# A gate/up stage that starts its first two products over four blocks instead of three, with their copies in one large tile

## The chip, the cores and the metric

The kernel runs on one core of one Trainium2 chip. The metric is the time of one execution on the device, in microseconds (us). The core has TensorE (matmuls into eight PSUM banks), VectorE, ScalarE, GpSimd and SyncE (SP), each with its own queue of instructions. DMA engines move data between HBM and SBUF.

## What is computed

One layer of a streaming encoder over 1024 tokens of width 1024: a SwiGLU feed-forward, a mixer of two head groups, a second feed-forward, and a final RMSNorm. The change touches the two feed-forwards alone, whose inner width is 2816:

```python
def _swiglu(x, w_gate, w_up, w_down):
    return (jax.nn.silu(x @ w_gate) * (x @ w_up)) @ w_down

h = _rmsnorm(x, ffn1_norm[l])
x = x + 0.5 * _swiglu(h, ffn1_w_gate[l], ffn1_w_up[l], ffn1_w_down[l])
# ... mixer ...
h = _rmsnorm(x, ffn2_norm[l])
x = x + 0.5 * _swiglu(h, ffn2_w_gate[l], ffn2_w_up[l], ffn2_w_down[l])
```

All is float32. A product of two float32 matrices is made of three matmuls, high by high, high by low and low by high, from operands that are split into a high half (a cast on ScalarE) and a low half (a subtraction on VectorE).

## The kernel before, in words

**Seven products.** The tokens are cut into two halves of 512 and the width into two halves of 512, so the normed input is four quarters A11, A12, A21, A22. Each pair of column blocks of a weight matrix is multiplied with it in seven products instead of eight (Strassen's scheme in Winograd's form). The inputs are A11, A12, A22 and the sums S1 = A21 + A22, S2 = S1 - A11, S3 = A22 - A21 (made as A22 - S2 after S2's update in place), S4 = A12 - S2. The products are numbered 1 to 7; the table at line 47 tells which input each takes: 1 A11, 2 A12, 3 S4, 4 A22, 5 S1, 6 S2, 7 S3.

**Blocks.** `gate_up` (L276) goes over 22 blocks: 11 pairs of columns, each first for the gate ("g"), then for up ("u"). A block has two weight rows of 0.5 MB (`row`, L287). `weight` (L299) makes the weights of one product from them: for products 1, 2 and 3 a split alone, for 5, 6, 7 and 4 a subtraction in place and then a split. `product` (L328) is 12 matmuls: four quarters of the inner width, three matmuls each. The blocks use PSUM banks by product: X for 1, 6, 7 and 4, which add up in one bank and are read after each; Z for 5 and 3; W for 2.

**Draining.** `evac` (L342) reads a bank after a product. After 1, 5 and 6 it copies it with ScalarE to an SBUF tile (L348). After 2, 3 and 7 VectorE adds bank and copy, in place in the copy (L362); a gate block's sum then goes through Silu, an up block's is multiplied with it (L368) and stored in HBM. After 4, `finish` (L375) makes the sums that the next stage reads.

**Order.** The list `steps` (L388) begins with product 1 of blocks 0 to 2, then product 2 of them, then 5, 6, 3, 7, 4 of them block by block; `early` is 3. From block 3 on, a block's seven products follow each other, with product 4 of the block before behind product 1. `run` (L395) goes through this list: it makes weights six steps ahead, issues the product, and drains it. With `hold=6` the first six products are not drained until the seventh step. The functions `s1`, `s2`, `s4`, `s3`, `a22` of `h_units` (L224) make the five late inputs; the list `STAGES` (L50) says at which steps they are issued. This order is the program's; the framework then places each engine's instructions by priority (the program's order) and by when it expects them to be ready, so that the order in a queue is fixed before the run but is not the text's.

**Buffers.** There are 14 large tiles ("big", four times 128x512), 17 tiles of 128x528 ("xt"), 5 weight rows ("raw"), 8 tiles of split weights ("unit") and 8 PSUM banks. The seven inputs take 14 large tiles when all are there, a high and a low one each. The two rows of block 2 lie in a large tile too (`extra`, L292), until its last weights have been made. The input x lies in 16 of the 17 xt tiles; x[0][0..3] come free after S2's subtractions (L257), x[0][4..7] after S4.

**After the gate/up stage** the down stage (`down`, L425) does the same with activations as inputs; it is not changed. Its loads are ordered behind the last product 1 of the gate/up stage.

Of the kernel before, what the change touches and what calls it, by code (L numbers as in the profile page):

```python
# [10 lines left out]
F32 = mybir.dt.float32  # L11
# [6 lines left out]
P = 128  # L18
D = 1024
S = 1024  # L20
T = 512
# [25 lines left out]
A_OF = {1: "A11", 2: "A12", 3: "S4", 4: "A22", 5: "S1", 6: "S2", 7: "S3"}  # L47
UNITS = ("A11", "A12", "A22", "S1", "S2", "S3", "S4")
GROUPS = ((0, 4), (4, 8), (8, 11))
STAGES = (5, 5, 7, 10, 12)  # L50


class Net:
# [222 lines left out]
    def gate_up(self, n):  # L276
        nc, d = self.nc, self.d
        self.actd = {
            (u, g): self.dp.tile([q1 - q0, P, T], F32, name=f"act{n}{u}{g}")
            for u in UNITS  # L280
            for g, (q0, q1) in enumerate(GROUPS)
        }
        blocks = [(p, m) for p in range(NP) for m in ("g", "u")]
        rows, sil, fence, extra = {}, {}, {}, []
        early = 3

        def row(b, i):  # L287
            p, m = blocks[b]
            if (b, i) not in rows:
                if b == early - 1:  # L290
                    if not extra:
                        extra.append(self.big.tile([P, 4, T], F32, tag="b", name=f"r{m}"))  # L292
                    rows[b, i] = extra[0][:, 2 * i : 2 * i + 2]
                else:
                    rows[b, i] = self.rp.tile([P, 2, T], F32, tag="r", name=f"r{m}{i}")
                nc.sync.dma_start(rows[b, i].rearrange("p a t -> p (a t)"), d[f"{m}{n}"][2 * p + i])
            return rows[b, i]

        def weight(b, M):  # L299
            r0 = row(b, 0)  # L300
            if M in (1, 2):
                src = r0[:, M - 1]
            else:
                r1 = row(b, 1)
                if M == 5:
                    src = r1[:, 0]
                    nc.vector.tensor_sub(src, r1[:, 0], r0[:, 0])
                elif M == 6:
                    src = r1[:, 0]
                    nc.vector.tensor_sub(src, r1[:, 1], r1[:, 0])  # L310
                elif M == 7:
                    src = r0[:, 0]
                    nc.vector.tensor_sub(src, r1[:, 0], r0[:, 0])
                elif M == 4:
                    src = r0[:, 1]
                    nc.vector.tensor_sub(src, r0[:, 1], r1[:, 0])
                else:
                    src = r1[:, 1]
            w = self.unit("wu")
            name = self.split(w[:, 0], w[:, 1], src, after=fence.get("early"))  # L320
            if (b, M) == (early - 1, 2):
                fence["early"] = name
            return w

        bank, part = {}, {}
        place = {1: "X", 6: "X", 7: "X", 4: "X", 5: "Z", 3: "Z", 2: "W"}

        def product(b, M, w):  # L328
            ch = place[M]
            new = M in (1, 2, 5)  # L330
            if new:
                bank[b, ch] = self.fpsum("p" + ch)
            ps = bank[b, ch]
            hh, hl = self.h[A_OF[M]]
            ins = self.mm3(
                ps, [(w[:, 0, k * P : k * P + P], w[:, 1, k * P : k * P + P], hh[:, k], hl[:, k]) for k in range(4)], start=new
            )
            self.last_mm = ins.ins.name
            if (b, M) == (len(blocks) - 1, 1):
                self.gate = self.last_mm  # L340

        def evac(b, M):  # L342
            p, m = blocks[b]
            ps = bank[b, place[M]]
            key = {1: "m1", 5: "m5", 6: "u2"}.get(M)
            if key:
                part[b, key] = self.tmp(key)
                nc.scalar.copy(part[b, key], ps)  # L348
                return
            if M == 4:  # L350
                if m == "g":
                    s = self.tmp("s21")
                    self.table(s, ps, AF.Silu)
                    sil[p, "A21"] = s
                else:
                    s = sil[p, "A21"]
                    nc.vector.tensor_mul(s, ps, s)
                    finish(p)
                return
            key, name = {2: ("m1", "A11"), 3: ("u2", "A12"), 7: ("m5", "A22")}[M]  # L360
            t = part.pop((b, key))
            nc.vector.tensor_add(t, ps, t)  # L362
            if m == "g":
                self.table(t, t, AF.Silu)
                sil[p, name] = t
            else:
                s = sil[p, name]
                nc.vector.tensor_mul(s, t, s)  # L368
                store(p, name, s)

        def store(p, u, t):
            g = next(i for i, (q0, q1) in enumerate(GROUPS) if q0 <= p < q1)
            nc.sync.dma_start(self.actd[u, g][p - GROUPS[g][0]], t)

        def finish(p):  # L375
            a11, a12, a21, a22 = (sil.pop((p, q)) for q in ("A11", "A12", "A21", "A22"))
            s1 = a21
            nc.vector.tensor_add(s1, a21, a22)
            store(p, "S1", s1)
            s2, s3, s4 = (self.tmp(q) for q in ("S2", "S3", "S4"))  # L380
            nc.vector.tensor_sub(s2, s1, a11)
            store(p, "S2", s2)
            nc.vector.tensor_sub(s3, a22, s2)
            store(p, "S3", s3)
            nc.vector.tensor_sub(s4, a12, s2)
            store(p, "S4", s4)

        steps = [(b, M) for M in (1, 2) for b in range(early)]  # L388
        steps += [(b, M) for M in (5, 6, 3, 7, 4) for b in range(early)][:-1]
        for b in range(early, len(blocks)):  # L390
            steps += [(b, 1), (b - 1, 4)] + [(b, M) for M in (2, 5, 6, 3, 7)]
        steps.append((len(blocks) - 1, 4))
        return steps, weight, product, evac

    def run(self, steps, weight, product, evac, ahead, hold=0, stages=(), at=(), early=()):  # L395
# [525 lines left out]
def layer(ctx, tc, d):  # L921
    net = Net(ctx, tc, d)
    nc = tc.nc
# [15 lines left out]
    with ExitStack() as f1:  # L939
        net.ffn_pools(f1)  # L940
        net.load_x(d["x"])
        r[0] = net.rsqrt(net.squares(0))
        ps = net.squares(1)
        first, kinds = net.h_units(0, r)
        first()
        r[1] = net.rsqrt(ps)
        net.run(*net.gate_up(1), ahead=6, hold=6, stages=list(zip(STAGES, kinds)))

        accs = [None, None]
        count = [0, 0]  # L950
        h = [None, None]

        pending = []

        def tail(c, k):
            if c and k < 4:
                pending.append(k)
                return
            finish(c, k)

        def finish(c, k):
            ins = nc.scalar.dma_start(x1[c, :, k], net.x[c][k])
            after = net.wcast["qk0"] if c and k < 4 else None
            if after:
                net.after(ins, after)
            accs[c] = net.square(net.x[c][k], accs[c], net.tmp, after)
            count[c] += 1
            if c == 0 and count[c] == KT:
                r[0] = net.rstd(accs[0], net.unit("sp"), net.fpsum)

        def early():
            h[0] = net.norm(0, 8, r[0], net.last_mm)

        net.down(1, d["x"], tail, order, ((4, 5), early))
# [34 lines left out]
    with ExitStack() as f2:  # L1009
# [5 lines left out]
            r2[1] = net.rsqrt(net.total(sums, net.fpsum, False))  # L1015

        stages = [(1, stats2)] + list(zip(STAGES, h2[1]))
        net.run(*net.gate_up(2), ahead=6, hold=6, stages=stages)

        accs3 = [None, None]  # L1020
        count3 = [0, 0]
# [82 lines left out]
```

## Time and profile before

| what | value |
|---|---|
| median of 3 runs | 1691.99 us (1691.86 to 1694.9) |
| the profiled execution | 1692.0 us, of which its span is 1690.2 us |
| mean granted clock of TensorE | 0.994 |
| TensorE matmuls busy | 1647.9 us, 97% |
| VectorE busy | 1110.1 us, 66% |
| ScalarE busy | 679.2 us, 40% |
| mean HBM traffic | 118 GB/s |

The profile is one execution. Times in a timeline are microseconds from the start of the span. PE is TensorE, DVE VectorE, ACT ScalarE, SP SyncE. A matmul's row is longer than the distance to the next one, since matmuls overlap in the pipeline and their ends are modelled: what a matmul costs is read from the distance between starts. A bracket behind a row tells how long the engine was idle before it and what it then waited for. Names in a row are the program's tiles: "pX<-A11h,wu" is a matmul into an X bank from the high half of A11 and a weight tile, "L212 ... wu<-rg,wu" the low half of a split.

### The profile page before, as it was taken

To read this page: it belongs to the slowest core of one execution; us is meant where nothing else is said; L and a number is where in the kernel's file an instruction comes from. 1 tells how busy PE (TensorE), PEld (TensorE's weight loads), DVE (VectorE), ACT (ScalarE), POOL (GpSimd) and SP (SyncE) were. 2 spreads that over 40 slices of the span, in tenths; PEclk is the share of its full clock that TensorE was granted. 3 is DMA by queue.
4 is the path that set the end of the run, shared out by engine and by line. 5 is a ranking of instruction groups with operands and counts; after the bars stand their busy time and mean duration, and the time that the engine had idled before them with its cause. 6 is when DMAs were issued, how large, how long until landed. Compare 5 with 4: busy or idle time off the path is not lost.

```text
span 1690.2 us, 19875 instructions
## 1 busy us (share of the span) xinstructions
PE 1647.9 (97%) x7314; PEld 1342.9 (79%) x7314; DVE 1110.1 (66%) x1771; ACT 679.2 (40%) x1155; POOL 60.5 (4%) x79
## 2 busy tenths in 40 slices
PE   6999999999999999999999999999999999999997
PEld 3688888888888877888877887788888888888875
DVE  7976565666569668942636539966666665579584
ACT  5643333333444445521423314633333333444452
POOL 0000000000000000100305200000000000000000
PEclk9999999999999999999999999999999999999998
DMA  5142322332795332230310342143233331893331
GB/s 187 61 139 94 106 100 94 112 101 81 246 329 187 110 113 89 61 95 13 106 38 13 121 166 75 69 132 105 100 105 102 111 119 57 279 326 111 112 119 50
DMA packets 95697, 200.07 MB, mean 118 GB/s; under 512 B 10472, under 2 KB 14568, under 8 KB 95600
## 3 DMA queue, kind: packets, MB, share of 16 engines
q1 hardware_dynamic: 89104, 187.21, 33.1%
q10 hardware_dynamic: 6496, 11.60, 1.8%
q8 instruction: 57, 0.93, 0.2%
q14 instruction: 40, 0.33, 0.1%
HBM read 145.78 MB, written 52.99 MB: 118 GB/s over the span
## 4 chain that ended last, share of the span: by engine, by line
PE 92%; DVE 5%; ACT 1%; DMA 1%; issue 1%; SPq 0%; DVEq 0%; ACTq 0%
PE pX L138 14%; PE pX L140 14%; PE pX L139 14%; PE pZ L139 7%; PE pZ L140 7%; PE pZ L138 7%; PE pW L138 3%; PE pW L139 3%; PE pW L140 3%; PE pg L140 3%; PE pg L138 3%; PE pg L139 3%; PE pt L593 2%; PE pt L594 2%; PE pt L592 2%; DVE x L236 1%
## 5 line engine op out<-in xcount | busy, mean ns | idle before, releaser
L209 ACT CAST au<-as 128x512 fp32r<-128x512 f32 x154 | 95.9, 623 | 208.1 <-PE pX L140 104.6
L212 DVE TENSOR_TENSOR au<-as,au 128x512 fp32r<-128x512 f32 x154 | 106.0, 688 | 108.5 <-ACT au L209 108.2
L212 DVE TENSOR_TENSOR wu<-rg,wu 128x512 fp32r<-128x512 f32 x154 | 106.0, 689 | 95.3 <-ACT wu L209 95.0
L209 ACT CAST wu<-ru 128x512 fp32r<-128x512 f32 x154 | 95.4, 622 | 154.9 <-PE pX L140 65.0
L212 DVE TENSOR_TENSOR wu<-ru,wu 128x512 fp32r<-128x512 f32 x154 | 105.6, 687 | 56.5 <-ACT wu L209 56.0
L138 PE MATMUL pX<-au,wu 128*128 128x512 f32 x352 | 137.2, 390 | 0.0
L209 ACT CAST wu<-rg 128x512 fp32r<-128x512 f32 x154 | 95.5, 621 | 103.3 <-issue 53.1
L139 PE MATMUL pX<-au,wu 128*128 128x512 f32 x352 | 137.0, 389 | 0.0
L140 PE MATMUL pX<-au,wu 128*128 128x512 f32 x352 | 137.0, 389 | 0.0
L212 DVE TENSOR_TENSOR wu<-wq,wu 128x512 fp32r<-128x512 f32 x154 | 105.0, 684 | 4.2 <-ACT wu L209 4.1
L209 ACT CAST wu<-wq 128x512 fp32r<-128x512 f32 x154 | 94.4, 615 | 7.6 <-DMA wq<-d 4.9
L138 PE MATMUL pX<-A11h,wu 128*128 128x512 f32 x176 | 70.1, 399 | 7.8 <-ACT wu L209 6.3
L138 PEld LDWEIGHTS pX<-au,wu 128*128 128x128 f32 x352 | 66.1, 188 | 14.3 <-ACT wu L209 0.7
L140 PEld LDWEIGHTS pX<-au,wu 128*128 128x128 f32 x352 | 66.1, 188 | 13.7
L139 PEld LDWEIGHTS pX<-au,wu 128*128 128x128 f32 x352 | 66.1, 188 | 13.7
L139 PE MATMUL pZ<-S1l,wu 128*128 128x512 f32 x176 | 69.4, 394 | 2.9 <-DVE S1l L212 2.9
L139 PE MATMUL pX<-A11l,wu 128*128 128x512 f32 x176 | 70.2, 399 | 0.9 <-DVE A11l L212 0.9
L138 PE MATMUL pX<-S2h,wu 128*128 128x512 f32 x176 | 68.7, 390 | 2.4 <-ACT m L348 2.4
L138 PE MATMUL pZ<-S1h,wu 128*128 128x512 f32 x176 | 68.0, 394 | 1.6 <-ACT S1h L209 1.3
L140 PE MATMUL pX<-A11h,wu 128*128 128x512 f32 x176 | 69.5, 396 | 0.0
L138 PE MATMUL pW<-A12h,wu 128*128 128x512 f32 x176 | 69.2, 393 | 0.0
L139 PE MATMUL pW<-A12l,wu 128*128 128x512 f32 x176 | 69.2, 393 | 0.0
(258 smaller groups left out, 4117.5 us busy)
## 6 DMA issues: line engine op xcount, KB each, us to landing
rg<-g SPq DMA_DIRECT2D x44, 512.0 KB, 3.6
ru<-u SPq DMA_DIRECT2D x44, 512.0 KB, 3.6
wq<-d SPq DMA_DIRECT2D x88, 256.0 KB, 5.2
x<-x SPq DMA_DIRECT2D x64, 256.0 KB, 5.3
as<-act1S SPq DMA_DIRECT2D x44, 256.0 KB, 3.4
as<-act2S SPq DMA_DIRECT2D x44, 256.0 KB, 3.3
act1S<-S SPq DMA_DIRECT2D x33, 256.0 KB, 2.1
as<-act1A SPq DMA_DIRECT2D x33, 256.0 KB, 4.5
```

The source lines that it names most:

```text
L138: nc.tensor.matmul(out, wh, hh, start=start and i == 0, stop=False, skip_group_check=True)
L139: nc.tensor.matmul(out, wh, hl, start=False, stop=False, skip_group_check=True)
L140: ins = nc.tensor.matmul(out, wl, hh, start=False, stop=stop and i == n - 1, skip_group_check=True)
L209: cast = nc.scalar.copy(hi, src)
L212: (eng or nc.vector).tensor_sub(lo, src, hi.bitcast(F32))
L236: nc.vector.scalar_tensor_tensor(x, x, g, r[c], op0=ALU.mult, op1=ALU.mult)
L592: nc.tensor.matmul(ps, hh, wh, start=k == 0, stop=False)
L593: nc.tensor.matmul(ps, hh, wl, start=False, stop=False)
L594: nc.tensor.matmul(ps, hl, wh, start=False, stop=k == KT - 1)
```

## The change

The early part grows by two products: products 1 and 2 of block 3 come behind those of blocks 0 to 2 and ahead of product 5 of block 0. From the later part they are taken out, so block 3 goes on with product 4 of block 2 and its own 5, 6, 3, 7. The order of later blocks stays.

Nothing is held back: `hold` is 0, and each product is drained when it is done. The copies of product 1 of blocks 0 to 3 go into four quarters of one large tile (`first`) and not into xt tiles. The adds of product 2 of these blocks read this copy and write a new xt tile.

The steps at which S2, S4, S3 and A22 are issued are moved by one or two (`STAGES`), and the mark that keeps later weights behind the early ones (`fence`) moves to product 2 of block 3.

```diff
-STAGES = (5, 5, 7, 10, 12)
+STAGES = (5, 6, 9, 12, 14)
...
-        rows, sil, fence, extra = {}, {}, {}, []
+        rows, sil, fence, extra, first = {}, {}, {}, [], []
         early = 3
...
-            if (b, M) == (early - 1, 2):
+            if (b, M) == (early, 2):
                 fence["early"] = name
...
             if key:
-                part[b, key] = self.tmp(key)
+                if M == 1 and b <= early:
+                    if not first:
+                        first.append(self.big.tile([P, 4, T], F32, tag="b", name="m"))
+                    part[b, key] = first[0][:, b]
+                else:
+                    part[b, key] = self.tmp(key)
                 nc.scalar.copy(part[b, key], ps)
                 return
...
-            t = part.pop((b, key))
-            nc.vector.tensor_add(t, ps, t)
+            t = src = part.pop((b, key))
+            if M == 2 and b <= early:
+                t = self.tmp("m1")
+            nc.vector.tensor_add(t, ps, src)
...
-        steps = [(b, M) for M in (1, 2) for b in range(early)]
+        steps = [(b, M) for M in (1, 2) for b in range(early)] + [(early, 1), (early, 2)]
         steps += [(b, M) for M in (5, 6, 3, 7, 4) for b in range(early)][:-1]
         for b in range(early, len(blocks)):
-            steps += [(b, 1), (b - 1, 4)] + [(b, M) for M in (2, 5, 6, 3, 7)]
+            steps += ([] if b == early else [(b, 1)]) + [(b - 1, 4)]
+            steps += [(b, M) for M in ((5, 6, 3, 7) if b == early else (2, 5, 6, 3, 7))]
...
-        net.run(*net.gate_up(1), ahead=6, hold=6, stages=list(zip(STAGES, kinds)))
+        net.run(*net.gate_up(1), ahead=6, hold=0, stages=list(zip(STAGES, kinds)))
...
-        net.run(*net.gate_up(2), ahead=6, hold=6, stages=stages)
+        net.run(*net.gate_up(2), ahead=6, hold=0, stages=stages)
```

## Rows read from the trace of the kernel before

**Rows 1.** The page, busy time: engine, us, share of the span, instructions.
```profile
PE 1647.9 (97%) x7314; PEld 1342.9 (79%) x7314; DVE 1110.1 (66%) x1771; ACT 679.2 (40%) x1155; POOL 60.5 (4%) x79
```

**Rows 2.** Busy time by stage: stretch, its length, engines, granted clock, DMA share, GB/s.
```profile
44.17:67.16 22.99, 18.86 (x73) 13.00 (x73) 22.77 (x38) 14.98 (x26) 0.00 (x0) 1.00 0.03 12
...
1053.58:1075.09 21.51, 18.64 (x74) 12.89 (x72) 21.31 (x36) 15.34 (x27) 0.00 (x0) 1.00 0.04 13
...
100.00:400.00 300.00, 300.00 (x1325) 248.47 (x1324) 185.62 (x285) 111.96 (x191) 0.00 (x0) 1.00 0.32 105
```

**Rows 3.** Timeline of TensorE, first feed-forward: start, length, instruction, count, idle before.
```profile
43.94 0.39 PE L140 MATMUL pW<-A12h,wu 128*128 128x512 f32 x1
45.61 0.73 PE L138 MATMUL pZ<-S1h,wu 128*128 128x512 f32 x2 [1.28 <-ACT S1h L209]
...
48.87 0.50 PE L139 MATMUL pZ<-S1l,wu 128*128 128x512 f32 x1 [0.54 <-DVE S1l L212]
...
56.15 0.50 PE L138 MATMUL pX<-S2h,wu 128*128 128x512 f32 x1 [1.22 <-ACT m L348]
...
67.16 0.39 PE L138 MATMUL pZ<-S4h,wu 128*128 128x512 f32 x1
...
75.32 0.39 PE L138 MATMUL pX<-S3h,wu 128*128 128x512 f32 x1
...
83.48 0.61 PE L138 MATMUL pX<-A22h,wu 128*128 128x512 f32 x2
83.94 0.39 PE L138 MATMUL pX<-A11h,wu 128*128 128x512 f32 x1
...
97.08 0.39 PE L138 MATMUL pZ<-S1h,wu 128*128 128x512 f32 x1
```

**Rows 4.** Timeline of TensorE, second feed-forward.
```profile
1033.73 0.80 PE L138 MATMUL pX<-A11h,wu 128*128 128x512 f32 x1 [3.35 <-ACT wu L209]
...
1040.15 0.39 PE L138 MATMUL pX<-A11h,wu 128*128 128x512 f32 x1
...
1053.58 0.61 PE L138 MATMUL pZ<-S1h,wu 128*128 128x512 f32 x2
...
1075.09 0.39 PE L138 MATMUL pZ<-S4h,wu 128*128 128x512 f32 x1
...
1105.01 0.39 PE L138 MATMUL pZ<-S1h,wu 128*128 128x512 f32 x1
```

**Rows 5.** Timeline of VectorE, first feed-forward.
```profile
41.57 2.07 DVE L236 SCALAR_TENSOR_TENSOR x<-x,cols,rstd 128x512 f32<-128x512 f32 x3
...
50.00 0.68 DVE L257 TENSOR_TENSOR x<-x,x 128x512 f32<-128x512 f32 x1
...
57.46 1.88 DVE L362 TENSOR_TENSOR m<-pW,m 128x512 f32<-128x512 f32 x3
...
83.60 2.49 DVE L212 TENSOR_TENSOR A22l<-x,A22h 128x512 fp32r<-128x512 f32 x4
86.00 0.68 DVE L362 TENSOR_TENSOR m<-pX,m 128x512 f32<-128x512 f32 x1
...
97.35 0.69 DVE L362 TENSOR_TENSOR m<-pW,m 128x512 f32<-128x512 f32 x1 [0.33 <-PE pW L140]
```

**Rows 6.** Timeline of ScalarE, first feed-forward.
```profile
42.16 0.62 ACT L209 CAST wu<-rg 128x512 fp32r<-128x512 f32 x1 [1.60 <-PE pW L140]
...
55.51 0.59 ACT L348 COPY m<-pX 128x512 f32<-128x512 f32 x1
```

**Rows 7.** Timeline of VectorE, second feed-forward.
```profile
1089.78 2.49 DVE L212 TENSOR_TENSOR A22l<-x,A22h 128x512 fp32r<-128x512 f32 x4
```

**Rows 8.** Busy time of a stretch, columns as in rows 2.
```profile
1034.00:1039.00 5.00, 5.00 (x12) 3.70 (x13) 5.00 (x9) 3.02 (x7) 0.00 (x0) 0.50 0.70 277
```

## The prediction

> **What bounds the kernel now.** I read the page first. TensorE is busy for 97% of the span and VectorE for 66% [rows 1], so the time can only fall where TensorE waits. The table by stage says where that is: in a steady stretch of the first gate/up, TensorE is busy for 300.00 of 300.00 us, but at the start of each gate/up it has real holes, and there VectorE is busy for all but 0.22 us of the stretch [rows 2]. Time gained there is gained at the end, for no hole follows until the stage is over.
>
> The size of the holes comes from the timeline of TensorE. With no hole, 36 matmuls (the three S4 products) take 75.32 - 67.16 = 8.16 us, that is 0.2267 us each and 2.72 us for a product of 12. In the first feed-forward the last early product starts its last matmul at 43.94, so TensorE is free at 44.17. The six products on S1 and S2 should take 16.32 us, but the first S4 matmul starts at 67.16: 22.99 us, so 6.67 us are lost [rows 3]. In the second feed-forward the same six run from 1053.58 to 1075.09, 21.51 us, so 5.19 us are lost [rows 4]. Together 11.86 us: more than this the change can't bring here.
>
> The timelines of VectorE and ScalarE tell why. VectorE begins the S1 chain (norm, add, split, for four quarters) only at 41.57 and works without a pause; S1's last quarter and S2 keep TensorE waiting in small steps [rows 3, 5]. Then (0,6) waits 1.22 us for a copy of the first product, made at 55.51 because the copies were held back and need a slot of the 17 [rows 3, 6].
>
> **The change part by part.** Write (b,M) for product M of block b.
>
> *Two products move forward.* (3,1) and (3,2) now run before S1 is needed. That is 24 matmuls, 5.44 us, in each feed-forward, put into holes of 6.67 and 5.19 us. Their weights cost VectorE one split each. The other two-step weights (difference and split) of (1,6) and (2,6) fall behind the S1 chain, so before S1 VectorE has 16 operations and not 18. Their weight row is no new transfer: five raw slots and the big tile of block 2 hold seven rows, and the seventh was block 3's first row already. It only goes ahead of the second rows of blocks 0 to 2 on SP's queue, 0.5 MB at a time when those are not yet wanted. Cost: nothing, as long as they land before the fifth products' differences.
>
> *Copies into a big tile.* Four copies on ScalarE, the same instructions as before, no longer wait for slots. This removes the 1.22 us wait of (0,6). ScalarE is busy for 14.98 of 22.99 us there [rows 2], so I cost them at nothing; if that cover went, they would cost four times 0.59 us [rows 6].
>
> *Adds at once.* The number of adds is the same, but their results need four new slots. Sixteen of 17 are x, so (0,2) takes the only spare one. (1,2) has to wait until the first S2 subtraction releases x[0][0]; that ran at 50.00 [rows 5]. This matters for banks: X0 to X3 and W0 to W3 are all eight, so (0,5) waits for the add of (0,2), (1,5) for that of (1,2), and so on. With S2's first quarter at about 50 to 51 and TensorE through with (3,2) at 44.17 + 5.44 = 49.6, (0,5) has two finished quarters of S1 to work on and the next bank comes free about 1 us later. I take that as filled.
>
> *Where the time gained meets the next wait.* The last input is A22's low half. It starts at 83.60 [rows 5], because the 14 big tiles are all taken until the weights of (2,4) give back the one with block 2's rows. Before, the displaced (3,1) was the cover here: TensorE began A22's products at 83.48, went over to A11 at 83.94, and reached (3,5) at 97.08 [rows 3]. After, that cover is gone. VectorE is full to this point, and what it must do before it is the same set (the weights of (3,1) and (3,2) already lay ahead of A22) plus two more: the add and the multiplication of (3,2), which before ran from 97.35 on [rows 5]. Four A22 splits take 86.00 - 83.60 = 2.40, so 0.60 us each, and two more make 1.20 us: A22's first low quarter ends at 83.60 + 1.20 + 0.60 = 85.40. Within one product the matmuls keep their order, so only the first of each of the three products can run earlier, and 33 remain: 7.48 us. (3,5) starts at 92.9, where before it was 97.08: **4.2 us**, although TensorE alone would allow 6.67. In the second feed-forward A22 starts at 1089.78 [rows 7]: 1089.78 + 1.80 + 7.48 = 1099.1 against 1105.01 [rows 4], 5.9 us, so here TensorE's own 5.19 is the limit: **5.2 us**. After (3,5) the weights are ready in time: VectorE had reached other work by 97.35, where it waits for TensorE for the first time.
>
> *What the adds can cost in VectorE's queue.* Before, VectorE read nothing of TensorE's in this stretch until 57.46 [rows 5]. After, the add of (0,2) stands ahead of the S1 chain, and behind it in the queue stand the whole chain, S2 and the splits; TensorE waits for those. The trace has no such wait on VectorE. The nearest row is ScalarE's cast at 42.16, which stood 1.60 us for a product of the same group [rows 6]: the fixed order expected TensorE earlier than it came. Bounds: zero (the add stands where TensorE is already done) and 1.6 us, and each microsecond moves A22 by one. A gain below zero I exclude, for the set of work is fixed. I take 1.0 us per feed-forward, nearer to the row of the same cause.
>
> Sum: 4.2 - 1.0 and 5.2 - 1.0 give 7.4 us. The profiled execution took 1692.0 us (span 1690.2 and 1.8 around it), the median of the runs is 1691.99, so no correction is due: **1684.6 us**.
>
> The Trainium skill's page "Perfetto Trace Analysis", section "Tensor Engine Instruction (MATMUL, LD_WEIGHTS)", states that ScalarE, VectorE and GpSimd are strict FIFO. By that rule an add that waits stops everything behind it, which speaks against draining at once and is the second rival below; its time would be 1691.0. The trace agrees as far as it goes: ScalarE stood 1.60 us at one cast with others behind it [rows 6].
>
> **The rivals.**
>
> *All holes filled.* Adds wait for nothing, and VectorE puts the four operations that drain the S4 products (three adds, one multiplication, 2.4 us) behind A22, so A22 comes no later than TensorE. Then both losses go: 1692.0 - 11.86 = 1680.1. For it: those four aren't needed by TensorE until block 3. Against it: before, they stood ahead of A22 though they could have stood behind.
>
> *VectorE's queue waits for TensorE.* Two adds stand too early: that of (0,2) by 3.0 us, since TensorE's start is late by about that (in the second feed-forward it waited 3.35 us and then ran 15 matmuls in 6.42 us at a granted clock of 0.50, that is 1.2 GHz, where 3.40 would do [rows 4, 8]), and that of (3,2) by the 1.6 us of the row above. Then 4.6 us are lost on VectorE: 4.2 - 4.6 = -0.4 and 5.9 - 4.6 = 1.3, together 0.9: 1691.0, no difference that can be told.
>
> *Banks run out: slower.* The adds of (1,2), (2,2) and (3,2) run only when S2 is done, as in the kernel before, where three ran from 57.46 [rows 5]; with five more operations of 0.60 us ahead that is 60.5, and the bank for (1,5) is free at 61.0. If TensorE's order holds (1,5) and (2,5) ahead of the S2 products, it has only (0,5) from 49.6 on and then five products, 13.6 us: S4 starts at 74.6, where 67.16 + 5.44 = 72.6 would be no change. That is 2.0 us lost, in one idle stretch longer than the one of 3.35 us, behind which TensorE ran at 1.2 GHz and lost 3.0 us [rows 4, 8]; with as much lost again, 5.0 us in each feed-forward, so 1702.0. It decides from the point where the add of (1,2) starts later than 72.6 - 13.6 = 59.0. For it: eight banks and one spare slot are all there is. Against it: the S2 products need no new bank and can go first (before, (0,6) went ahead of (2,5)), and S2's first subtraction ran at 50.00, before S1 was complete.
>
> **How the numbers follow.** A measurement of this kernel can tell about 0.2%, 3.4 us, from no change. The forecast (1681 to 1688) has 0.48, all holes filled 0.20, the waiting queue 0.20, the banks 0.12. Faster: 0.48 + 0.20 = 0.68; same 0.20; slower 0.12. The range from 1680.1 to 1691.0 takes in the first three cases with the bounds of the waits (0 and 1.6 us each), and leaves the banks out.
>
> **What would show it.** In the profile after: (3,1) and (3,2) end near 49.6, with no hole of more than 0.7 us between them and S4; the wait for the copy at L348 is gone; the first S4 matmul is near 67, as before, but with two more products behind it; the low half of A22 starts near 85 to 86; (3,5) starts near 94 and its twin near 1101. A wait of VectorE for pW between 36 and 50 of over 2 us would show the second rival, a wait of TensorE for a drain of pW, and a granted clock of 0.50 after it, the third. The forecast is wrong if VectorE idles in this stretch, or if A22 is not what TensorE waits for last.

## The result, and the profile after

| what | before | after |
|---|---|---|
| median, runs side by side (five of each) | 1693.06 us (1691.86 to 1695.86) | 1684.8 us (1684.21 to 1685.14) |
| ratio, with its 95% interval | | 0.9949 [0.9938, 0.9959] |
| the profiled execution, its span | 1692.0 us, 1690.2 us | 1684.21 us, 1682.4 us |
| mean granted clock | 0.994 | 0.995 |

The changed kernel is faster by 0.5%. The forecast was 1684.6 us. The time is right, but some of the steps that lead to it are not. To see that, the stage has to be measured again in the same way as before.

The page first: busy time by engine, as in [rows 1].

```profile
PE 1644.3 (98%) x7314; PEld 1343.0 (80%) x7314; DVE 1108.1 (66%) x1771; ACT 680.9 (40%) x1155; POOL 60.4 (4%) x79
```

The instructions are the same in number; only their order differs. Next the busy time by stage, as in [rows 2]: from the end of the six early products of the first feed-forward to its first S4 matmul, and inside it the stretch in which the fifth product of block 0 runs.

```profile
44.78:69.19 24.41, 22.62 (x97) 17.86 (x96) 24.41 (x41) 14.04 (x24) 0.00 (x0) 1.00 0.06 22
50.22:55.56 5.34, 3.55 (x13) 2.09 (x12) 5.34 (x10) 3.00 (x5) 0.00 (x0) 1.00 0.00 0
```

VectorE is busy for all of it, and TensorE idles for a third of the short stretch. The timeline of TensorE, first feed-forward, answers to [rows 3].

```profile
44.55 0.39 PE L140 MATMUL pW<-A12h,wu 128*128 128x512 f32 x1
...
49.99 0.39 PE L140 MATMUL pW<-A12h,wu 128*128 128x512 f32 x1
50.22 0.39 PE L138 MATMUL pZ<-S1h,wu 128*128 128x512 f32 x1
...
52.58 0.50 PE L139 MATMUL pZ<-S1l,wu 128*128 128x512 f32 x1 [0.62 <-DVE S1l L212]
...
53.84 0.50 PE L138 MATMUL pZ<-S1h,wu 128*128 128x512 f32 x1 [0.52 <-ACT S1h L209]
54.99 0.50 PE L139 MATMUL pZ<-S1l,wu 128*128 128x512 f32 x1 [0.65 <-DVE S1l L212]
...
55.56 0.40 PE L138 MATMUL pX<-S2h,wu 128*128 128x512 f32 x1
55.80 0.39 PE L138 MATMUL pZ<-S1h,wu 128*128 128x512 f32 x1
...
69.19 0.39 PE L138 MATMUL pZ<-S4h,wu 128*128 128x512 f32 x1
...
85.52 0.39 PE L138 MATMUL pX<-A22h,wu 128*128 128x512 f32 x1
86.28 0.50 PE L139 MATMUL pX<-A22l,wu 128*128 128x512 f32 x1 [0.37 <-DVE A22l L212]
...
95.02 0.39 PE L138 MATMUL pZ<-S1h,wu 128*128 128x512 f32 x1
```

The six early products end at 44.55 + 0.23 = 44.78, and (3,1) and (3,2) follow at once, to 50.22. From 44.78 to the first S4 matmul there are 24.41 us for eight products of 2.72 us, 21.76: 2.66 us are lost, where [rows 3] lost 6.67. From S4 to A22 72 matmuls take 16.33 us: nothing is lost. Then the first matmul on A22's low half comes 0.76 us after the one before it and the next 0.33 us after that, where 0.23 each would do: 0.66 us are lost, and before there was nothing here. The same in the second feed-forward, beside [rows 4]:

```profile
1030.30 0.60 PE L138 MATMUL pX<-A11h,wu 128*128 128x512 f32 x1 [3.35 <-ACT wu L209]
...
1034.16 0.39 PE L138 MATMUL pX<-A11h,wu 128*128 128x512 f32 x1
...
1048.72 0.39 PE L140 MATMUL pW<-A12h,wu 128*128 128x512 f32 x1
...
1057.84 0.50 PE L139 MATMUL pZ<-S1l,wu 128*128 128x512 f32 x1 [0.65 <-DVE S1l L212]
...
1072.03 0.39 PE L138 MATMUL pZ<-S4h,wu 128*128 128x512 f32 x1
...
1088.35 0.39 PE L138 MATMUL pX<-A22h,wu 128*128 128x512 f32 x1
1089.12 0.50 PE L139 MATMUL pX<-A22l,wu 128*128 128x512 f32 x1 [0.39 <-DVE A22l L212]
```

From 1048.95 to 1072.03 are 23.08 us, so 1.32 us are lost before S4, none up to A22, and 0.68 there (three small gaps). This table collects the losses; "hole" is the one before S4, the last column is up to the fifth product of block 4.

| us lost | first: hole | at S4 to A22 | behind A22 | sum | second: hole | at S4 to A22 | behind A22 | sum |
|---|---|---|---|---|---|---|---|---|
| before | 6.67 | 0 | 0.01 | 6.68 | 5.18 | 0 | 0 | 5.18 |
| after | 2.66 | 0 | 0.66 | 3.31 | 1.32 | 0 | 0.68 | 1.99 |

The stage gained 3.37 and 3.19 us, 6.56 together. The two spans differ by 7.8 us. Of the rest 1.20 us is in the start of the second feed-forward: behind the same pause of 3.35 us, TensorE ran 15 matmuls in 6.42 us before [rows 4, 8] and nine in 3.86 us after, that is 3.02 and 1.82 us more than at 0.2267 each. Most of this is not the change's: see the part on the sum, and the section on the hardware.

VectorE, beside [rows 5] and [rows 7] (the last two rows are the second feed-forward):

```profile
39.31 0.69 DVE L212 TENSOR_TENSOR wu<-rg,wu 128x512 fp32r<-128x512 f32 x1 [1.31 <-ACT wu L209]
...
40.52 0.68 DVE L369 TENSOR_TENSOR m<-pW,m 128x512 f32<-128x512 f32 x1
...
42.33 2.07 DVE L236 SCALAR_TENSOR_TENSOR x<-x,cols,rstd 128x512 f32<-128x512 f32 x3
...
53.65 0.68 DVE L257 TENSOR_TENSOR x<-x,x 128x512 f32<-128x512 f32 x1
...
54.86 0.68 DVE L369 TENSOR_TENSOR m<-pW,m 128x512 f32<-128x512 f32 x1
...
85.53 2.50 DVE L212 TENSOR_TENSOR A22l<-x,A22h 128x512 fp32r<-128x512 f32 x4
...
1038.92 0.69 DVE L212 TENSOR_TENSOR wu<-ru,wu 128x512 fp32r<-128x512 f32 x1 [2.40 <-ACT wu L209]
...
1088.39 2.48 DVE L212 TENSOR_TENSOR A22l<-x,A22h 128x512 fp32r<-128x512 f32 x4
```

The add of (0,2) (40.52) waits for nothing. VectorE waits ahead of it, for a cast. S2's first subtraction is at 53.65, where it was at 50.00, and the add of (1,2) comes behind it. A22's low half starts at the very moment at which TensorE wants it, in both feed-forwards. ScalarE, beside [rows 6], shows what the cast waited for:

```profile
35.90 0.59 ACT L353 COPY m<-pX 128x512 f32<-128x512 f32 x1 [4.00 <-PE pX L140]
38.17 0.59 ACT L353 COPY m<-pX 128x512 f32<-128x512 f32 x1 [1.69 <-PE pX L140]
38.66 0.62 ACT L209 CAST wu<-rg 128x512 fp32r<-128x512 f32 x1
```

The copies of (0,1) and (1,1) stand in ScalarE's queue until TensorE has made their products. The cast behind them starts at 38.66, and VectorE's split of the same weights at 39.31.

### The profile page after: what moved, and what is told of

Read it like the earlier page. It is cut to its first block, busy times and chain, and to the rows that moved or that the text cites. A ratio compares the mean times of both kernels' runs of the same rounds, so it can differ in the third digit from the quotient of the medians.

```text
span 1682.4 us, 19872 instructions
## 1 busy us (share of the span) xinstructions
PE 1644.3 (98%) x7314; PEld 1343.0 (80%) x7314; DVE 1108.1 (66%) x1771; ACT 680.9 (40%) x1155; POOL 60.4 (4%) x79
## 4 chain that ended last, share of the span: by engine, by line
PE 89%; DVE 9%; ACT 1%; issue 1%; DMA 1%; SPq 0%; DVEq 0%; ACTq 0%
PE pX L138 13%; PE pX L139 13%; PE pX L140 13%; PE pZ L138 6%; PE pZ L139 6%; PE pZ L140 6%; PE pW L138 3%; PE pW L139 3%; PE pW L140 3%; PE pg L140 3%; PE pg L138 3%; PE pg L139 3%; PE pt L601 2%; PE pt L602 2%; PE pt L600 2%; DVE x L236 1%
## 5 line engine op out<-in xcount | busy, mean ns | idle before, releaser
L139 PE MATMUL pX<-A22l,wu 128*128 128x512 f32 x176 | 68.7, 390 | 0.8 <-DVE A22l L212 0.8
```

Source lines behind the costliest of these rows:

```text
L139: nc.tensor.matmul(out, wh, hl, start=False, stop=False, skip_group_check=True)
```

## The experiments

Each edit is given against the changed kernel unless it says otherwise. The table at the end has the losses of all, worked out as above.

**The drains alone.** How much is the draining worth without the two products? The kernel before, with its three blocks, gets `hold=0` and the large tile:

```diff
-                part[b, key] = self.tmp(key)
+                if M == 1 and b < early:
...
+                    part[b, key] = first[0][:, b]
+                else:
+                    part[b, key] = self.tmp(key)
...
+            if M == 2 and b < early:
+                t = self.tmp("m1")
...
-        net.run(*net.gate_up(1), ahead=6, hold=6, stages=list(zip(STAGES, kinds)))
+        net.run(*net.gate_up(1), ahead=6, hold=0, stages=list(zip(STAGES, kinds)))
```

> The kernel before with the second half of the change alone: products 1 and 2 over three blocks as before, but each bank drained at once and the copies in a large tile. Theory (the gain is in the two products that fill the hole, up to the point where VectorE has A22 ready): only the wait of 1.22 us for the copy at L348 goes, in each feed-forward, so 1690 us (1689 to 1692). Rival (the gain comes from draining at once, which frees banks and slots): most of the 7.8 us, so about 1686 us.

Measured: 1689.26 us against 1693.01 for the kernel before, ratio 0.9971 [0.9961, 0.9980]. The losses fall from 6.68 to 5.39 and from 5.18 to 2.25. So the drains alone bring 4.2 us of the 6.6 in the profiles, more in the second feed-forward (2.93 us) than the 1.22 us of the copy that I had named. The median lies where the theory of this run put it, but the losses speak for its rival: most of the gain comes from draining at once. Almost nothing is lost at A22, since (3,1) is still there as its cover.

**No large tile.** Copies go into xt tiles and the adds stay in place, with all the rest of the change kept:

```diff
-                if M == 1 and b <= early:
+                if False:
...
-            if M == 2 and b <= early:
+            if False:
```

> The changed kernel without the large tile: four blocks in the early part and nothing held back, but the copies of product 1 go into xt tiles and the adds are in place, as before. Theory (the order carries the gain, the slots come free with S2 in both): the copies of blocks 1 to 3 wait for S2's subtractions and each add waits one copy more, 0.6 us; 1685 to 1687 us. Rival (the large tile is what lets the banks go): (1,5) and (2,5) come later by several us and the gain is lost, 1690 us or more.

Measured: 1683.31 us, ratio 0.9943 [0.9928, 0.9958]; losses of 3.28 and 1.56. The large tile isn't needed for the gain; both expectations had put this run at a later time. The place of the wait is what this run teaches. VectorE's and then ScalarE's timeline of it, first feed-forward:

```profile
39.89 0.69 DVE L369 TENSOR_TENSOR m<-pW,m 128x512 f32<-128x512 f32 x1 [1.19 <-PE pW L140]
...
36.33 0.62 ACT L209 CAST wu<-rg 128x512 fp32r<-128x512 f32 x1 [4.94 <-DVE rg L307]
```

No copy stands ahead of the cast here; VectorE waits at the add of (0,2), for 1.19 us, as the prediction had it. With the tile it waits 1.31 us for a cast instead. One wait takes the place of the other.

**Is A22 on VectorE the wall now?** S3's low half is computed twice, four more subtractions of 0.60 us (2.4 us of VectorE in each feed-forward) ahead of A22, once in the changed kernel and once in the kernel before:

```diff
+                hi, lo = self.h["S3"]
+                nc.vector.tensor_sub(lo[:, k], a21, hi[:, k].bitcast(F32))
```

> The changed kernel with four more VectorE operations in each feed-forward: the low halves of S3 are computed twice. Four times 0.60 us is 2.4 us in each. Theory (VectorE's work up to A22 sets when block 3 goes on; no cover is left): A22's low half comes 2.4 us later and all of it is seen, 4.0 to 4.8 us, so 1688.8 to 1689.6 us. Rival (what remains is TensorE waiting for banks behind S1, VectorE has room at A22): under 1 us, 1685 us.

> The kernel before with the same four more VectorE operations in each feed-forward. Theory (there the products 1 and 2 of block 3 stood behind A22's start and cover 5.44 us): A22 comes 2.4 us later but TensorE has (3,1) and (3,2) to run, so no change, 1692 to 1693 us. Rival (VectorE was the bound before too, by the same amount): 4.0 to 4.8 us more, 1696 to 1697 us.

Measured: in the changed kernel 1692.03 us (ratio 0.9988 [0.9978, 0.9997]), about 7 us more; in the kernel before 1692.51 us (0.9995 [0.9985, 1.0004]), no change. The timeline of VectorE and the waits of TensorE (from 20 to 100 us; total, times, longest) in the changed kernel with the four:

```profile
87.83 2.49 DVE L212 TENSOR_TENSOR A22l<-x,A22h 128x512 fp32r<-128x512 f32 x4
...
PE pX L138 <- DVE m L371: 1.3, 1, 1.3
PE pX L139 <- DVE A22l L212: 1.2, 1, 1.2
```

This settles that the cover is gone: the same 2.4 us cost nothing at A22 where (3,1) and (3,2) run beside it, and are paid in full where they don't, 2.43 us in the second feed-forward and 3.97 us in the first. (In the kernel before, the second hole is 0.67 us larger; in that execution TensorE was through with the early products 18.38 us after their start and not 19.85, so it waited longer for S1.) The row of 1.3 us is part of both payments: the add that frees the X bank comes late as well. What the first feed-forward overpays, about 1.5 us, is the clock: behind the waits of 1.3 and 1.2 us seven matmuls, which at 0.2267 each would take 1.59 us, took 3.15 us at a granted clock of 0.50 (columns as in [rows 2]).

```profile
88.58:91.73 3.15, 3.15 (x8) 2.48 (x8) 3.15 (x6) 1.08 (x3) 0.00 (x0) 0.50 0.66 268
```

**The S3 subtractions on GpSimd.** If VectorE is the wall, moving four operations away should give back the 0.66 us:

```diff
-                put("S3", k, a21)
+                put("S3", k, a21, nc.gpsimd)
```

> The changed kernel, but the four low halves of S3 are computed by GpSimd (1.25 us each in the mixer), so VectorE has 2.4 us less to do before A22 in each feed-forward. Theory: A22 comes 2.4 us earlier, but TensorE comes to A22 only at 85.5, so only the wait at A22 goes, 0.4 to 0.7 us in each: 1683.4 to 1684.4 us. Rival (VectorE's total work alone sets the time): 4 to 4.8 us less, about 1680.3 us. If GpSimd slows VectorE, 1685 us or more.

Measured: 1688.58 us, ratio 0.9973 [0.9963, 0.9984]: slower than the changed kernel. The loss at A22 is gone, but 2.2 us are lost at S3 in each feed-forward. GpSimd's timeline, then VectorE's beside it:

```profile
72.54 9.11 POOL L212 TENSOR_TENSOR S3l<-x,S3h 128x512 fp32r<-128x512 f32 x4 [70.89 <-ACT S3h L209]
...
75.34 0.68 DVE L369 TENSOR_TENSOR u<-pZ,u 128x512 f32<-128x512 f32 x1
75.94 1.20 DVE L316 TENSOR_TENSOR rg<-rg,rg 128x512 f32<-128x512 f32 x1
77.06 1.78 DVE L212 TENSOR_TENSOR wu<-rg,wu 128x512 fp32r<-128x512 f32 x1
78.76 0.68 DVE L369 TENSOR_TENSOR u<-pZ,u 128x512 f32<-128x512 f32 x1
79.36 1.16 DVE L212 TENSOR_TENSOR wu<-rg,wu 128x512 fp32r<-128x512 f32 x1
80.44 1.76 DVE L375 TENSOR_TENSOR u<-u,u 128x512 f32<-128x512 f32 x1
```

My price for one was 1.25 us, from the mixer, where the rows show 1.30 on average. Here the four took 9.11 us, and VectorE's own operations became longer too. The theory of the wall isn't touched by this; the price was wrong.

**Adds of the up blocks in place.** The add of (1,2) waits for a slot that S2's first subtraction frees. An up block's sum can stay in the large tile (a gate block's goes to HBM from there later, so it can't without holding the tile):

```diff
-            if M == 2 and b <= early:
+            if M == 2 and b <= early and m == "g":
```

> The changed kernel, but the add of product 2 of blocks 1 and 3 (the up blocks) is written over its copy in the large tile, so it needs no xt slot and the bank for (1,5) is free as soon as (1,2) is done. In the changed kernel (0,5) runs alone behind S1's quarters until 55.3 and the hole before S4 is 2.65 us (first) and 1.32 us (second feed-forward). Theory (VectorE's A22 is the next wall and stands just behind): TensorE gains in the S1 stretch and waits as much at A22, so at most 1.3 us, 1683.5 to 1684.8 us. Rival (the banks are what is left): 3 to 4 us less, about 1681 us.

Measured: 1685.55 us, 0.9955 [0.9940, 0.9970]. The hole shrinks from 2.66 to 1.96 and from 1.32 to 0.20, so at least 0.70 and 1.12 us of it were the slot and the bank behind it (S1's chain began 1.5 and 0.9 us later in this run, counted from TensorE's first matmul, and the hole shrank even so). But A22 starts later, at 86.02 on VectorE, which is 65.38 us behind the first matmul instead of 64.06, and what was gained before S4 is lost again from S4 on: the sums are 3.94 and 2.16. Since A22 itself moved, this run alone doesn't show that an A22 in its old place would have eaten the gain.

**Both of the last two.** 

> Both edits of the two kernels beside it: the add of up blocks in place, and S3's low halves on GpSimd. Theory (two walls of nearly the same time, banks at S1 and VectorE at A22): alone each brings about 0.5 to 1.3 us, together 3.5 to 5 us, so 1680 to 1681.3 us. Rival (each edit counts for itself): the sum of what the two brought alone.

Measured: 1688.48 us, 0.9972 [0.9962, 0.9982]. The hole is that of the adds in place, the rest the price of GpSimd, so this run can't tell whether there are two walls.

**Copies later.** To take the copies from the head of ScalarE's queue, their issue was put three steps later:

```diff
-            if i < hold:
-                held.append((b, M))
+            if late and i < 3:
+                held.append((i + 3, (b, M)))
...
+                for step in [s for at_, s in held if at_ <= i]:
+                    evac(*step)
...
```

> The changed kernel, but the copies of product 1 of blocks 0 to 2 are issued three steps later, so that on ScalarE they stand behind the casts of later weights. In the changed kernel ScalarE waited 4.00 and 1.69 us for TensorE at two of these copies, and VectorE then 1.31 us (first) and 2.40 us (second feed-forward) for a cast behind them. Theory: VectorE's whole chain moves 1.3 us and 2.4 us earlier, S1 and A22 both with it, so 1.3 to 2.5 us less in all: 1682.3 to 1683.5 us. Rival (VectorE waits for the add of product 2 in the same place instead): 1684.8 us.

Measured: 1685.31 us, 0.9955 [0.9940, 0.9969]. This one is inconclusive, for the order of the queue stayed as it was. ScalarE's timeline, then VectorE's:

```profile
35.72 0.59 ACT L353 COPY m<-pX 128x512 f32<-128x512 f32 x1 [5.12 <-PE pX L140]
38.01 0.59 ACT L353 COPY m<-pX 128x512 f32<-128x512 f32 x1 [1.70 <-PE pX L140]
...
39.15 0.69 DVE L212 TENSOR_TENSOR wu<-rg,wu 128x512 fp32r<-128x512 f32 x1 [2.44 <-ACT wu L209]
```

The copies kept their places, presumably because the framework places by when it expects an instruction to be ready; no run tests that. What the gain would be without that wait is not known. In effect this run is the changed kernel once more, in an execution with more half clock (see the run before the table).

**Drains of the S4 products behind A22.** The first rival needed VectorE to put three adds and a multiplication behind A22. Here the text does so: product 3 of blocks 0 to 2 is drained only behind product 7 of block 2.

```diff
-            if i < hold:
+            if M == 3 and b < hold:
                 held.append((b, M))
...
-            if i == hold:
+            if (b, M) == (hold - 1, 7):
...
-        net.run(*net.gate_up(1), ahead=6, hold=0, stages=list(zip(STAGES, kinds)))
+        net.run(*net.gate_up(1), ahead=6, hold=3, stages=list(zip(STAGES, kinds)))
...
```

> The changed kernel, but the drains of the S4 products of blocks 0 to 2 (three adds, a multiplication: 2.4 us of VectorE, nothing that TensorE needs before block 3's fourth bank) are issued behind the S3 products, so that A22's low half can go ahead of them. Theory (A22 on VectorE and TensorE's arrival are two walls at nearly the same time): A22 is ready 2.4 us earlier, TensorE comes no earlier than 85.5, so only the wait at A22 goes, 0.4 to 0.7 us in each feed-forward: 1683.4 to 1684.4 us. Rival (VectorE alone): 4 to 4.8 us less, 1680 to 1681 us.

Measured: 1683.54 us, 0.9948 [0.9932, 0.9965]; beside it, on the same chip, the changed kernel itself 1685.43 us, 0.9955 [0.9940, 0.9970]:

> The changed kernel itself, beside these three on the same chip, so that differences of one or two us can be read. Expected: 1684.8 us, as before; what the chip changes, it changes for all.

The intervals overlap; the profiles are plainer. VectorE's timeline with the drains moved:

```profile
82.97 2.49 DVE L212 TENSOR_TENSOR A22l<-x,A22h 128x512 fp32r<-128x512 f32 x4
...
88.98 1.87 DVE L369 TENSOR_TENSOR u<-pZ,u 128x512 f32<-128x512 f32 x3
```

A22 comes 2.56 us earlier than at 85.53; 0.95 of that is this execution's earlier begin (first matmul at 20.52, not 21.47), so 1.61 us are the edit's. The three adds stand behind it, and the loss at A22 is gone in both feed-forwards: 2.64 and 1.34 instead of 3.31 and 1.99. Again the losses end where TensorE, not VectorE, is the limit: of 1.61 us only 0.66 are gained.

**Both: drains behind A22 and adds in place.**

> As the kernel with the late S4 drains, and the adds of the up blocks in place. In place alone took 0.69 and 1.12 us from the hole before S4 and gave 1.04 and 1.27 us back at A22. Theory: with A22 2.4 us earlier nothing is given back, so 1.8 us less than the changed kernel from S1 and 1.3 us from A22, 3 us together: 1681.5 to 1682.5 us. Rival (A22 is bound by the slot that block 2's rows hold, not by VectorE's work): no earlier than with in place alone, 1685 us.

Measured: 1681.69 us (1680.91 to 1682.38), 0.9933 [0.9918, 0.9948], 3.7 us less than the changed kernel on the same chip. This beats both kernels. Busy time by stage, from the end of the six early products to its first S4 matmul, second feed-forward:

```profile
1047.78:1069.74 21.96, 21.96 (x97) 17.80 (x96) 21.96 (x37) 12.79 (x23) 0.00 (x0) 1.00 0.07 25
```

TensorE is busy for all of it; by the starts of eight products, 21.76 us, 0.20 us are lost here, and 1.96 us still in the first feed-forward. By the medians, adds in place alone brought nothing, the later drains alone 1.9 us, both 3.7. Part of that is the clock, which differs between executions; by the losses it is -0.8, 1.3 and 2.6 us. Either way, what comes sooner before S4 is worth nothing until A22 comes sooner too.

**The later drains without the large tile.** 

> The kernel without the large tile (1683.3 us), with the late S4 drains. There TensorE reached A22 at 85.21 and VectorE had begun it at 84.92, so by the theory there is no wait left to take: 1682.8 to 1683.5 us. Rival (VectorE alone): 1679 to 1680 us.

Measured: 1683.69 us, 0.9945 [0.9930, 0.9960], against 1683.31 without the drains moved (other chip). As expected the medians show no further gain: there the adds are in place and A22 was nearly on time (0.37 and 0.40 us lost). The profile is of the slowest of this run's four executions, and its first hole is larger, 4.17 us, as in the run with the copies later (4.28, also its slowest of four). Busy time and clock behind S1's waits tell why, for the copies later and then for this run:

```profile
54.83:58.34 3.51, 3.51 (x8) 2.75 (x9) 3.51 (x7) 1.75 (x3) 0.00 (x0) 0.51 0.21 77
...
55.41:58.80 3.39, 3.39 (x8) 2.57 (x9) 3.17 (x6) 2.44 (x5) 0.00 (x0) 0.54 0.06 23
```

Eight matmuls took 3.51 and 3.39 us, where 8 x 0.2267 = 1.81 would do. So 1.7 and 1.6 us of these two holes are half clock and not the order of the kernel. Without it this run's losses would be about 3.7 us against the 4.84 without the drains moved, an estimate, so a gain of about 1 us may hide behind the clock here.

| us lost | first: hole | S4 to A22 | behind A22 | sum | second: hole | S4 to A22 | behind A22 | sum |
|---|---|---|---|---|---|---|---|---|
| drains alone | 5.29 | 0.02 | 0.08 | 5.39 | 2.20 | 0.05 | 0 | 2.25 |
| no large tile | 2.91 | 0 | 0.37 | 3.28 | 1.16 | 0 | 0.40 | 1.56 |
| after, four more | 2.68 | 1.42 | 3.18 | 7.28 | 1.35 | 1.44 | 1.64 | 4.42 |
| before, four more | 6.68 | 0 | 0.02 | 6.70 | 5.86 | 0 | 0 | 5.85 |
| S3 on GpSimd | 2.68 | 2.18 | 0 | 4.86 | 1.32 | 2.20 | 0 | 3.52 |
| adds in place | 1.96 | 0.52 | 1.46 | 3.94 | 0.20 | 0.24 | 1.72 | 2.16 |
| GpSimd, in place | 1.96 | 3.62 | 0 | 5.58 | 0.20 | 3.38 | 0 | 3.57 |
| copies later | 4.28 | 0 | 0 | 4.27 | 0.83 | 0 | 0.68 | 1.50 |
| drains behind A22 | 2.65 | 0 | 0 | 2.64 | 1.34 | 0 | 0 | 1.34 |
| the same, in place | 1.96 | 0.30 | 0 | 2.26 | 0.20 | 0 | 0.31 | 0.50 |
| the same, no tile | 4.17 | 0 | 0 | 4.16 | 1.12 | 0 | 0 | 1.12 |
| after, again | 2.66 | 0 | 0.67 | 3.33 | 1.34 | 0 | 0.67 | 2.00 |

## Why the prediction was right, and where it was not

**What bounds the kernel** was right: of the two holes of 6.67 and 5.18 us the change could take no more, and the gain of 6.56 us in the stages is what the holes gave (7.87) less what is now lost at A22 (1.3). That VectorE had slack at A22 before is shown by the kernel before with four more subtractions, which stayed at its time.

**Which half of the change pays.** The prediction gave the draining no more than the wait of 1.22 us and looked for the gain in the two products. By the run with the drains alone, the draining brings 1.29 and 2.93 us of the 3.37 and 3.19, and the two products add 2.08 us in the first feed-forward and 0.26 in the second. The forecast didn't suffer, for it took the gain of both halves together, up to A22.

**Two products into the holes.** They ran without a gap, to 50.22 (forecast 49.6; the stage began 0.57 us later, with its first matmul at 21.47 and not at 20.90). But the holes were not filled: 2.66 and 1.32 us are left, and S4 starts at 69.19 where "near 67" was forecast. The step that failed is "I take that as filled": that (0,5) would have two quarters to work on and the next bank about 1 us later. It had the two quarters, but S1's last two came one by one (gaps of 0.62, 0.52, 0.65 us), and the bank for (1,5) came some 5 us later, with the add of (1,2) at 54.86. That add needs the slot from S2's first subtraction, which was forecast for 50 to 51 and came at 53.65, with two splits, a difference and S1's last sum ahead of it. The bank and slot are at least 0.70 and 1.12 us of the holes by the run with the adds in place; the 1.96 us that are left in the first in that run are TensorE waiting for S1's low halves, so VectorE's. No single gap in the brackets is over 0.65 us, so by them the sign I had named (a hole of over 0.7 us) would have missed it; by the starts, the next matmul came up to 0.93 us too late. The sum was to be looked at.

**Copies at nothing.** The wait of TensorE for a copy is gone, as forecast. But the copies weren't free: I looked at how busy ScalarE is, not at what stands behind a copy in its queue. They stood 4.00 and 1.69 us, and VectorE waited 1.31 us for the cast behind them (2.40 us in the second). The Trainium skill, "Perfetto Trace Analysis", section "Tensor Engine Instruction (MATMUL, LD_WEIGHTS)", has ScalarE and VectorE as strict FIFO; these rows agree, and the rule should have been applied to the copies as it was to the adds.

**The queue's price, 1.0 us, and the two operations, 1.20 us.** Together they should have put A22 off by 2.2 us. Counted from TensorE's first matmul, to leave out the later begin, it came 64.06 - 62.70 = 1.36 us later in the first feed-forward and 58.09 - 56.05 = 2.04 us in the second. Busy time from that matmul to A22, two rows of before and two of after (columns as in [rows 2], VectorE the third number behind the length):

```profile
20.90:83.60 62.70, 54.49 (x217) 40.97 (x218) 62.42 (x104) 36.37 (x63) 0.00 (x0) 0.97 0.15 48
1033.73:1089.78 56.05, 53.18 (x211) 41.02 (x212) 55.04 (x91) 34.60 (x61) 0.00 (x0) 0.94 0.20 71
...
21.47:85.53 64.06, 58.17 (x241) 45.89 (x241) 62.75 (x104) 37.75 (x64) 0.00 (x0) 0.97 0.12 36
1030.30:1088.39 58.09, 57.34 (x243) 46.35 (x243) 55.28 (x93) 35.81 (x61) 0.00 (x0) 0.97 0.17 58
```

VectorE idled for 0.28 and 1.01 us before, and for 1.31 and 2.81 us after. So the new waiting is 1.03 us in the first feed-forward, as priced, and 1.80 in the second, over the upper bound of 1.6. Its place was wrong: it was put at the add of (0,2), but with the large tile that add waits for nothing, and VectorE waits for the cast behind the copies (without the tile the add does wait, 1.19 us). And "the same set plus two more" was wrong: busy time grew by 0.33 and 0.24 us, not by 1.20, for the add of (1,7), which before ran ahead of A22 (81.19), now runs behind it (88.55).

**The wall at A22.** This is the step that carried the forecast, and it held: A22's low half is what TensorE waits for last (0.37 and 0.39 us in one gap), (3,5) has its rest from 95.02 (forecast "near 94", plus the begin), four more operations on VectorE cost 2.4 us in each feed-forward (and 1.5 us of half clock in the first), and the drains put behind A22 take the loss away. That in the second feed-forward TensorE's own 5.19 us would be the limit was wrong: A22 (1088.39) is met there too, and the gain of the stage is 3.19 us instead of the 4.2 forecast. In the first it is 3.37 instead of 3.2.

**Why the sum is right all the same.** 7.4 us were forecast. The stages gave 6.56 us, and the shorter start of the second feed-forward 1.20 us. Some 0.8 us of the latter would have come to the kernel before as well: in its order, early products and hole took 19.85 + 5.18 = 25.03 us in one execution and 18.38 + 5.86 = 24.24 us in another. So the change is worth about 7 us in these profiles, an estimate; in executions of equal mean granted clock, on another chip, it is 7.2 to 7.5 us (last section), and the medians differ by 8.3 us. That it comes close to the forecast is no accident: the hole left open (2.66 and 1.32 us) is mostly hidden, because A22 would not have been ready sooner, and this hid the error in the fill. That it hits the measured median to 0.2 us is luck: A22 was 0.84 and 0.16 us less late than forecast, 35 matmuls and not 33 remained behind its first low quarter, since only one ran ahead (85.52), which cost 0.45 us each time, the second limit was misplaced, and the clock did the rest.

**The rivals.** All holes filled: its mechanism is real (the drains behind A22 gain 0.66 us in each), but the framework left the drains ahead of A22, and without the in-place adds it is worth 1.3 us, not 4. VectorE's queue: no wait of over 2 us at an add, and not the time; but its mechanism is there by another way, for VectorE waited 2.40 us in the second feed-forward for a cast that stood behind a copy of TensorE's result. Banks: the add of (1,2) at 54.86 is ahead of the 59.0 from which it decides; the bank was late, but not by enough. The clock that this rival feared stayed at 1.00 in the half-idle stretch of this profile; in two others with the same order of products it fell to 0.51 and 0.54 behind it and cost 1.7 and 1.6 us.

## What to carry to other kernels

A hole filled ahead of an engine that is full shows at the next input that this engine makes; so ask for each input behind the hole what covered it before, and test it by adding work to that engine in both kernels. An engine that is 40% busy isn't free for an instruction that reads another engine's result: look at what stands behind that in its queue. What removes two limits in a row doesn't add up from its parts: the two repairs gained nothing and 1.9 us alone, and 3.7 together. Look at the clock of a stretch before comparing two profiles of it: it can be worth as much as the change.

## What the runs showed of the hardware

**GpSimd beside a full VectorE.** The four subtractions took 4.04, 1.74, 1.72 and 1.72 us, where the same shape took 1.30 on average in the mixer of the kernel before, and VectorE's operations that read two operands in SBUF took 1.16 to 1.78 us beside the last three, instead of 0.68. The one beside these that reads PSUM (78.76) took 0.68. The Trainium skill, "GPSIMD Engine Reference", section "Specifications", says that GpSimd shares its SBUF interfaces with VectorE, with contention for instructions with two SBUF inputs; these rows agree. It has the same operation on GpSimd at about twice VectorE's time (section "Engine selection"); the 1.30 us of the mixer are 1.9 times 0.68 and agree, but beside the full VectorE it was 2.5 times, and 5.9 times for the first.

**The clock behind a pause.** Behind the same pause of 3.35 us TensorE ran 15 matmuls at half clock in one execution and eight or nine in another. It goes with the execution, not with the kernel's order: the stretch from the first matmul to the end of the six early products of the second feed-forward took 19.85 and 18.38 us in two profiles with the order of before (the kernel itself, and with four more subtractions), and 18.64 and 19.79 in two with that of after (the same two). The times follow the mean granted clock in part. On one chip, the kernel before took 1693.2 us in an execution at 0.994 and 1691.6 (two) at 0.996, and the changed kernel 1685.7 (three) at 0.994 and 1684.4 at 0.996: 7.5 and 7.2 us apart. But three executions of the kernel before at 0.995 took from 1692.0 to 1694.2 us.

**The clock behind short waits.** In the changed kernel's profile TensorE waited 0.62, 0.52 and 0.65 us between 51 and 55 us and stayed at a granted clock of 1.00. In the run with the copies later it waited 0.61, 0.52 and 0.66 us in the same place, and its next eight matmuls ran at 0.51, which is the lower level, 1.2 GHz. So the same waits can cost 1.7 us more in one execution than in another.
